# A diffusion layer on one Trainium2 core: sums of squares and weight block sums given to VectorE

## The chip, the cores and the metric

The kernel runs on one core of one Trainium2 chip. The time is the device's microseconds (us) for one execution; lower is better. All engines of the core are used: TensorE (PE, with its weight loads PEld), VectorE (DVE), ScalarE (ACT), GpSimd (POOL), and SyncE (SP), which issues most of the DMA transfers.

## What is computed

One layer of a hybrid diffusion backbone, in float32, for 1024 latent tokens and 256 context tokens of 1024 channels:

```python
def rms_norm(x, g):
    return x * lax.rsqrt(jnp.mean(x * x, axis=-1, keepdims=True) + EPS) * g

def swiglu(h, w_in, w_out):                      # w_in 1024 x 5632, w_out 2816 x 1024
    a, b = jnp.split(h @ w_in, 2, axis=-1)
    return (jax.nn.silu(a) * b) @ w_out

x = x + 0.5 * g1 * swiglu(modulate(rms_norm(x, n1), s1, c1), ffn1_w_in, ffn1_w_out)
h = modulate(rms_norm(x, n2), s2, c2)
...                                              # h @ w_in; short convolution; attention; merge; w_out
x = x + 0.5 * g3 * swiglu(modulate(rms_norm(x, n3), s3, c3), ffn2_w_in, ffn2_w_out)
out = rms_norm(x, final_g)                       # the output: latent tokens only
```

The context tokens pass through the first two parts with the same weights. What matters here are the norms (each needs, per token, the sum of the squares of its 1024 channels) and the two products with `w_out` of the feed-forward parts.

## The kernel before, in words

Activations lie transposed: a tile is 128 channels by 512 tokens, so the 1024 latent tokens are two chunks, C0 and C1, of eight tiles each. All instructions go through wrappers of one line (L90), so a profile's line column always says L90 and groups are told by the names of their tiles. A tile framework schedules the instructions, so that neighbours in the program need not be neighbours on an engine.

**The stages.** FFN1 (input product, SwiGLU; the hidden values `hid` go to DRAM and come back), FFN1's output product, the mixer's input products, attention, the merge, `w_out`, FFN2's input product, FFN2's output product with the final norm, and the output.

**The output products, `row_products`.** The product of `w_out` with the hidden values is taken as seven products over 2x2 blocks (Strassen's scheme), in the order 2, 1, 4, 6, 5, 7, 3. Its `groups` are six steps over the 11 k-tiles of 128 rows: five steps of two k-tiles (tiles of 128x2x512) and a last one of a single k-tile (128x512). `operands` yields both factors of a step, each split into a high part rounded by ScalarE (`wh`/`wl` of the weights and `rh` of the hidden values) and the rest, which VectorE makes by a subtraction; the weights' high and low parts lie in the tiles `wl`/`wh` by turns, and the hidden values' in `rh`/`rl`. Each k-tile then takes 12 matmuls of 128x512: four column blocks by three pairs of parts. Three products use sums of weight blocks as their weights: product 5 `s1[k]` = w12 + w22, product 6 `s2[k]` = w11 − s1, and product 3 the same tile with w21 added. `sums(i, g)` makes them ahead of time. For every group the quarter w12 is loaded by SP into a tile `ws`, and GpSimd issues a DMA that adds w22 to it in SBUF (`plus`, an accumulating DMA). In product 4, ScalarE copies −s1 into another tile `ws`, and GpSimd issues a DMA that adds w11 to that; in product 6 a third adds w21 for product 3. Groups 0 to 2 get their s1 in product 1, and groups 3 to 5 in product 4. So GpSimd has three such DMAs per group, 18 in each of the two `row_products`; it issues them in order, and an accumulating DMA follows the one before it once that has landed. Product 4's own weights are w22, in a tile `raw` (three buffers) loaded by `part_of_w`. `halves=True` (FFN2) takes product 3 in two halves of 256 tokens at the end.

**The norms.** ScalarE squares each of the eight channel tiles of a chunk. `square` adds the squares 0 to 6 into one tile, `sq_acc`, by VectorE, and keeps the eighth, `sq`, apart. `rstd_cols` then multiplies each 128 tokens of each such tile with a column of ones on PE (`pt<-ones,sq`, a product of 128x1 that is summed in PSUM), VectorE makes the reciprocal root of it (`rs_a`, `rs_t`, `rs_y`), and `bcast` spreads it by transposes (`ident,rs_y`). `square` serves the mixer's norm of C0 and of C1, and FFN2's norm of C1.

**The end, `final`.** It is called for three chunks of tokens: 512 (C0), 256, and the last 256 (`early`). Of the eight squares of a chunk, C0 adds them in pairs to four tiles; the two others add the first four in pairs and keep the other four, which makes six. Each of these is multiplied with ones for each 128 tokens: 4x4 + 2x6 + 2x6 = 40 products with ones. The values themselves (`yf`) are transposed by PE, scaled by VectorE or ScalarE into `ot`, and stored. `after3` places these steps between the matmuls of FFN2's product 3.

Of the kernel before, what the change touches and what calls it, by code (L numbers as in the profile page):

```python
# [12 lines left out]
AF = mybir.ActivationFunctionType  # L13
# [5 lines left out]
P = 128  # L19
D = 1024  # L20
KD = D // P
# [30 lines left out]
def tile_dit_layer(  # L52
# [44 lines left out]
    act, dve, pool, pe, sp = (Engine(e) for e in (nc.scalar, nc.vector, nc.gpsimd, nc.tensor, nc.sync))  # L97
# [15 lines left out]
    def atile(name, shape=(P, SLOT), dt=F32):  # L113
        return apool.tile(list(shape), dt, tag="A", name=uniq(name))
# [377 lines left out]
    class Winograd:  # L492
# [53 lines left out]
        def square(self, d, ch=C1):  # L546

            accs, n = self.accs.setdefault(ch, []), self.n_squares.get(ch, 0)
            sq = ttile("sq" if n else "sq_acc")
            act.activation(out=sq, in_=self.xs(d, ch), func=AF.Square)  # L550
            if n in (0, KD - 1):
                accs.append(sq)
            else:
                dve.tensor_add(out=accs[0], in0=accs[0], in1=sq)
            self.n_squares[ch] = n + 1
# [270 lines left out]
    def row_products(w, rows, add, after=lambda i, k: None, halves=False):  # L826
# [9 lines left out]


        R, groups = P * rows.n, rows.groups
        s1, s2 = {}, {}

        def block(k, m, lower, right):
            o = k * P + R * lower
# [2 lines left out]
        def part_of_w(*kmlr):  # L845
            t = wpool.tile([P, 2, 512], F32, tag="raw", name=uniq("raw"), bufs=3)[:, : kmlr[1]]
            load(t, block(*kmlr))
            return t

        def plus(t, *kmlr):  # L850
            pool.dma_start(out=t, in_=block(*kmlr), accum_op=ALU.add)
# [14 lines left out]
        def blocks(k):  # L866
            return (rows.t[k, v, c] for v in range(2) for c in range(2))

        def fetches(i, g):
# [5 lines left out]
            elif i == 1:  # L875
                rows.fetch(0, 0, g + 5)
                rows.fetch(0, 1, g + 2)

        def sums(i, g):

            n = len(groups)
            if i == 2 and g >= 2 or i == 1 and g < 2:
                k, _ = groups[g - 2 if i == 2 else n - 2 + g]
                _, _, b21, b22 = blocks(k)
                dve.tensor_sub(out=b21, in0=b21, in1=b22)
            if i == 1 and g or i == 4 and g == 0:
                k, _ = groups[g - 1 if i == 1 else n - 1]
                b11, b12, b21, _ = blocks(k)
                dve.tensor_sub(out=b11, in0=b12, in1=b11)
                dve.tensor_add(out=b21, in0=b21, in1=b11)  # L890
            if i == 1 and g >= 3 or i == 4 and g < n - 3:
                k, m = groups[g - 3 if i == 1 else n - 3 + g]
                s1[k] = atile("ws", (P, 2, 512))[:, :m]
                load(s1[k], block(k, m, 0, 1))
                plus(s1[k], k, m, 1, 1)
            k, m = groups[g]
            b11, b12, _, b22 = blocks(k)
            if i == 4:
                dve.tensor_sub(out=b11, in0=b11, in1=b22)
                s2[k] = atile("ws", (P, 2, 512))[:, :m]  # L900
                act.activation(out=s2[k], in_=s1[k], func=AF.Copy, scale=-1.0)
                plus(s2[k], k, m, 0, 0)
            elif i == 6:
                dve.tensor_add(out=b11, in0=b11, in1=b22)
                plus(s2[k], k, m, 1, 0)
            elif i == 5:
                dve.tensor_sub(out=b12, in0=b22, in1=b12)

        def operands(i, k, m):

            b11, b12, b21, b22 = blocks(k)
            if i in (1, 2, 4):
                left = part_of_w(k, m, i != 1, i == 4)
            elif i == 7:
                left, a21 = part_of_w(k, m, 0, 0), part_of_w(k, m, 0, 1)
                dve.tensor_sub(out=left, in0=left, in1=a21)
            else:
                left = (s1 if i == 5 else s2)[k]
            right = {1: b11, 2: b21, 4: b21, 5: b11, 6: b11, 7: b12, 3: b22}[i]
            for e in range(m):  # L920
                if i != 3:
                    where = ("wl", "wh")[(k + e) % 2], "t"
                else:
                    where = ("kept", "kept") if halves else ("wl", "wh")
                yield parts(left[:, e], where[0]), parts(right[:, e], where[1])
# [150 lines left out]
    for k in range(4):  # L1076
        if k % 2:
            half1.shifted(h0[k][:, 0], k, xh[k])
        else:
            dve.tensor_scalar(  # L1080
                out=h0[k][:, 0], in0=xh[k], scalar1=gain1["l"][:, k : k + 1], scalar2=modl[:, k : k + 1],
# [158 lines left out]
    for d in range(0, KD, 2):  # L1240
# [8 lines left out]
        for e in range(2):  # L1249
            te = t[:, e * CT : (e + 1) * CT]  # L1250
            dve.scalar_tensor_tensor(
                out=te, in0=pt[:, e * CT : (e + 1) * CT], scalar=gate1["c"][:, d + e : d + e + 1], in1=te, op0=ALU.mult, op1=ALU.add
# [78 lines left out]
    for i in range(KD):  # L1331
# [6 lines left out]
        for ch, bg, gc in mixed():  # L1338
# [4 lines left out]
            for j in (0, 2):  # L1343
# [3 lines left out]
                    out=ya, in0=u[:, a + j - 1 : b + j - 1], scalar=col(f"w{j}", i), in1=ya, op0=ALU.mult, op1=ALU.add  # L1347
# [383 lines left out]
    for ch in (C0, C1):  # L1731
        o = ch[1]
        for d in range(KD):
# [7 lines left out]
                out=xs(d, ch), in0=ps, scalar=modl[:, 40 + d : 41 + d], in1=xs(d, ch), op0=ALU.mult, op1=ALU.add  # L1741
# [12 lines left out]
        out=gf[:], in0=cols[:, voff["gf"] : voff["gf"] + 8], scalar1=math.sqrt(D), scalar2=None, op0=ALU.mult  # L1754
    )
    def final(ch, order, early=False):

        s, o, n = ch
        sqs, yk, turned = [], {}, {}
        for i, k in enumerate(order):  # L1760
            sq = ttile("sq", n)
            act.activation(out=sq, in_=xs(k, ch), func=AF.Square)
            if i % 2 and (i < 4 or n == 512):
                dve.tensor_add(out=sq, in0=sq, in1=sqs.pop())
            sqs.append(sq)
            if i % 2 == 0:
                y2 = atile("yf", (P, 2, 512))
            yk[k] = y2[:, k % 2, :n]
            dve.tensor_scalar(out=yk[k], in0=xs(k, ch), scalar1=gf[:, k : k + 1], scalar2=None, op0=ALU.mult)
            yield  # L1770

        def turn(j, half):
            pt = (ps_o if half and not early else ps_s)()
            for i in range(4):
                transpose(pt[:, i * P : (i + 1) * P], yk[half * 4 + i][:, j * P : (j + 1) * P], pinned=early)
            return pt

        if early:
            turned = {(j, half): turn(j, half) for half in (1, 0) for j in range(n // P)}
        rstd = rstd_cols(sqs, n, D)  # L1780
        yield
        for j in range(n // P):
            ot = atile("ot")
            for half in range(2):
                pt = turned.get((j, half)) or turn(j, half)
                oh = ot[:, half * 512 : (half + 1) * 512]
                if half:
                    act.activation(out=oh, in_=pt, func=AF.Copy, scale=rstd[:, j : j + 1])
                else:
                    dve.tensor_scalar(out=oh, in0=pt, scalar1=rstd[:, j : j + 1], scalar2=None, op0=ALU.mult)  # L1790
            sp.dma_start(out=out[0, o + j * P : o + (j + 1) * P, :], in_=ot[:])
            yield
# [94 lines left out]
```

## Time and profile before

| | |
|---|---|
| time, median of 3 runs | 2662.51 us (2657.9 to 2662.89) |
| the profiled execution's own time | 2661.18 us |
| its span in the profile | 2659.4 us |
| mean granted TensorE clock | 0.995 |
| DRAM read and written | 308.88 MB and 69.76 MB |

Times are us unless marked ns. In a group of instructions, "out<-in" are the program's names of the tiles, then shape and count; behind the bar stand busy time and mean ns of one, and behind the second bar the engine's idle time just ahead of them and what ended it. A timeline row gives start and duration, and in brackets the idle time just ahead and the instruction that ended it. The chain of waits is the work that ended last, followed back from the end; in it "issue" is time in which an engine waited for nothing that the profile shows. A table by windows gives for each stretch the busy time and count of each engine, the granted TensorE clock as a share of full speed, the DMA's share and GB/s. One product with ones stands in the trace as two records.

### The profile page before, as it was taken

How to read it: one execution, taken by the hardware profiler on the slowest of the kernel's cores; microseconds unless marked ns; L12 is line 12 of the kernel's file. 1: busy time of each engine (PE TensorE's matmuls, PEld its weight loads, DVE VectorE, ACT ScalarE, POOL GpSimd, SP SyncE). 2: the span in 40 equal slices, each digit the busy share in tenths (PEclk: the TensorE clock that was granted, in tenths of full speed). 3: DMA queues.
4: the chain of work that ended last, by engine and by line, in shares of the span. 5: the costliest groups of instructions: out<-in, count | busy, mean ns of one | idle time of the engine just before them, and what ended most of it. 6: DMA issues, size and time to landing. Idle time of an engine off the chain costs nothing.

```text
span 2659.4 us, 35547 instructions
## 1 busy us (share of the span) xinstructions
PE 2625.4 (99%) x12749; PEld 2187.9 (82%) x12749; DVE 1996.4 (75%) x3361; ACT 1170.4 (44%) x2321; POOL 556.7 (21%) x431
## 2 busy tenths in 40 slices
PE   8999999999999999999999999999999999999998
PEld 6788899888778878888888888888888888888888
DVE  5778976878887899877788676675458876667895
ACT  6533454433443642333345576574235333334453
POOL 0143201221010044333023112141001533230200
PEclk9999999999999999999999999999999999999999
DMA  8656465345974455332522432113525643227841
GB/s 320 203 180 204 139 222 174 108 127 189 323 181 111 130 178 164 115 123 88 192 78 94 91 89 64 32 48 104 162 81 182 190 147 99 80 91 284 187 91 64
DMA packets 368394, 381.03 MB, mean 143 GB/s; under 512 B 19526, under 2 KB 252120, under 8 KB 368216
## 3 DMA queue, kind: packets, MB, share of 16 engines
q1 hardware_dynamic: 357400, 357.22, 41.4%
q0 software_dynamic: 10816, 21.53, 4.9%
q8 instruction: 100, 1.64, 0.3%
q14 instruction: 78, 0.64, 0.1%
HBM read 308.88 MB, written 69.76 MB: 142 GB/s over the span
## 4 chain that ended last, share of the span: by engine, by line
PE 89%; DVE 5%; issue 2%; DMA 2%; ACT 1%; POOL 0%; SPq 0%; DVEq 0%; ACTq 0%; POOLq 0%
PE ps L90 74%; PE po L90 8%; PE pt L90 7%; DVE wl L90 1%; DMA rawm<-in_w_mod_dram 1%; DVE macc L90 0%; DVE r L90 0%; DVE xb L90 0%; DVE nt L90 0%; DVE u L90 0%; DMA xtok<-in_x_dram 0%; DVE rs_t L90 0%; POOL ws L90 0%; DMA ws<-in_ffn_w_out_dram 0%; DVE y L90 0%
## 5 line engine op out<-in xcount | busy, mean ns | idle before, releaser
L90 PE MATMUL ps<-r,wl 128*128 128x512 f32 x5196 | 1204.2, 391 | 6.2 <-DVE wl L90 3.7
L90 PEld LDWEIGHTS ps<-r,wl 128*128 128x128 f32 x5196 | 974.5, 188 | 211.8 <-DVE wl L90 5.4
L90 ACT CAST wl<-raw 128x512 fp32r<-128x512 f32 x287 | 177.6, 619 | 222.5 <-PE ps L90 177.0
L90 ACT CAST wl<-sum 128x512 fp32r<-128x512 f32 x218 | 133.4, 619 | 300.5 <-PE ps L90 221.9
L90 DVE TENSOR_TENSOR wl<-raw,wl 128x512 fp32r<-128x512 f32 x287 | 202.3, 707 | 60.1 <-ACT wl L90 58.5
L90 DVE TENSOR_TENSOR wl<-sum,wl 128x512 fp32r<-128x512 f32 x218 | 195.8, 899 | 31.4 <-ACT wl L90 30.3
L90 POOL TENSOR_TENSOR sum<-raw 128x512 f32<-128x512 f32 x55 | 77.5, 1409 | 665.8 <-DMA raw<-in_w_in_dram 203.9
L90 DVE SCALAR_TENSOR_TENSOR macc<-rawm,silu_c,macc 128x512 f32<-128x512 f32 x178 | 144.9, 832 | 16.0 <-DMA rawm<-in_w_mod_dram 15.5
L90 DVE TENSOR_TENSOR u<-u,ps 128x512 f32<-128x512 f32 x186 | 126.0, 679 | 38.2 <-PE ps L90 38.2
L90 POOL TENSOR_TENSOR sum<-raw,sum 128x512 f32<-128x512 f32 x55 | 80.5, 1464 | 311.0 <-DVE wl L90 311.0
L90 DVE TENSOR_TENSOR pts<-pt,pts 128x512 fp32r<-128x512 f32 x160 | 108.7, 686 | 44.2 <-ACT pts L90 42.5
L90 ACT CAST pts<-pt 128x512 fp32r<-128x512 f32 x160 | 93.2, 594 | 86.7 <-PE pt L90 81.7
L90 DVE TENSOR_REDUCE m<-ps 128x1 f32<-128x512 f32 (+1 forms) x192 | 110.2, 594 | 22.0 <-PE ps L90 21.0
L90 ACT CAST rh<-hid 128x512 fp32r<-128x512 f32 x132 | 81.3, 619 | 100.3 <-PE ps L90 88.5
L90 PE MATMUL ps<-rh,wl 128*128 128x512 f32 x360 | 122.2, 390 | 2.1 <-ACT rh L90 2.1
L90 PE MATMUL ps<-wh,r 128*128 128x512 f32 x384 | 120.7, 392 | 0.0
L90 ACT CAST wh<-raw 128x512 fp32r<-128x512 f32 (+1 forms) x85 | 67.8, 801 | 104.0 <-PE ps L90 74.2
L90 PE MATMUL po<-pts,vh 128*128 128x512 f32 x256 | 110.0, 435 | 0.2 <-ACT pts L90 0.2
L90 DVE TENSOR_TENSOR rl<-hid,rh 128x512 fp32r<-128x512 f32 x132 | 89.9, 684 | 22.6 <-PE ps L90 11.0
L90 PE MATMUL ps<-kl,qs 128*128 128x512 f32 x384 | 104.2, 395 | 0.0
L90 PE MATMUL ps<-rh,wh 128*128 128x512 f32 x300 | 102.3, 389 | 0.0
L90 POOL DMA_DIRECT2D ws<-in_ffn_w_out_dram x36 | 42.3, 1257 | 275.7 <-PE ps L90 85.9
(317 smaller groups left out, 5147.4 us busy)
## 6 DMA issues: line engine op xcount, KB each, us to landing
raw<-in_ffn_w_in_dram SPq DMA_DIRECT2D x130, 512.0 KB
raw<-in_ffn_w_out_dram SPq DMA_DIRECT2D x72, 512.0 KB
raw<-in_w_in_dram SPq DMA_DIRECT2D x61, 512.0 KB
rawm<-in_w_mod_dram SPq DMA_DIRECT2D x104, 256.0 KB
hid<-hd SPq DMA_DIRECT2D x40, 512.0 KB
rawm<-in_w_mod_dram SPq DMA_DIRECT2D x32, 512.0 KB
ws<-in_ffn_w_out_dram POOLq DMA_DIRECT2D x30, 512.0 KB, 6.5
ucd<-uc SPq DMA_DIRECT2D x29, 512.0 KB
```

The source lines that it names most:

```text
L90: inst = getattr(self.engine, name)(*args, **kw)
```

## The change

Three edits, each to sums.

In `square` the eighth square is also added by VectorE, so that each norm has one accumulator where it had two, and four products with ones where it had eight, at three uses.

In `final` all squares of a chunk are added into one tile; the early chunk keeps the last square apart. The products with ones go from 40 to 10 (4x1 + 2x1 + 2x2), VectorE's additions from 8 to 20: three more of 128x512 and nine more of 128x256.

In `row_products` the sum w12 + w22 of the groups 3 to 5 is made by VectorE from product 4's raw tile, where GpSimd's accumulating DMA made it before; that tile holds w22 (`part_of_w(k, m, 1, 1)` in product 4), though the change names it `w11`. −s1 of these groups, with the DMA behind it, is issued one group later, the last one in product 6. GpSimd has 15 accumulating DMAs per call where it had 18, and VectorE three additions more, two of 128x1024 and one of 128x512.

```diff
@@ square
-            if n in (0, KD - 1):
+            if n == 0:
                 accs.append(sq)
             else:
                 dve.tensor_add(out=accs[0], in0=accs[0], in1=sq)
@@ row_products
+        def second_sum(k, m):
+            s2[k] = atile("ws", (P, 2, 512))[:, :m]
+            act.activation(out=s2[k], in_=s1[k], func=AF.Copy, scale=-1.0)
+            plus(s2[k], k, m, 0, 0)
@@ sums(i, g)
                 load(s1[k], block(k, m, 0, 1))
-                plus(s1[k], k, m, 1, 1)
+                if i == 1:
+                    plus(s1[k], k, m, 1, 1)
             k, m = groups[g]
+            if i == 4 and g >= n - 3:
+                dve.tensor_add(out=s1[k], in0=s1[k], in1=w11.pop(k))
             b11, b12, _, b22 = blocks(k)
             if i == 4:
                 dve.tensor_sub(out=b11, in0=b11, in1=b22)
-                s2[k] = atile("ws", (P, 2, 512))[:, :m]
-                act.activation(out=s2[k], in_=s1[k], func=AF.Copy, scale=-1.0)
-                plus(s2[k], k, m, 0, 0)
+                if g < n - 3:
+                    second_sum(k, m)
+                elif g > n - 3:
+                    second_sum(*groups[g - 1])
             elif i == 6:
+                if g == 0:
+                    second_sum(*groups[n - 1])
                 dve.tensor_add(out=b11, in0=b11, in1=b22)
                 plus(s2[k], k, m, 1, 0)
@@ operands, i in (1, 2, 4)
                 left = part_of_w(k, m, i != 1, i == 4)
+                if i == 4:
+                    w11[k] = left
@@ final
             act.activation(out=sq, in_=xs(k, ch), func=AF.Square)
-            if i % 2 and (i < 4 or n == 512):
-                dve.tensor_add(out=sq, in0=sq, in1=sqs.pop())
-            sqs.append(sq)
+            if i and not (early and i == KD - 1):
+                dve.tensor_add(out=sqs[0], in0=sqs[0], in1=sq)
+            else:
+                sqs.append(sq)
```

**GpSimd, FFN1's output product.** These are its accumulating DMAs from the fourth on, before; ws_7020, ws_7067 and ws_7116 are the sums s1 of groups 3 to 5, and the others −s1 and what is added to it, of groups 0 to 5.

```order
L90 DMA ws_7020<-in_ffn_w_out_dram 128x2x512
L90 DMA ws_7024<-in_ffn_w_out_dram 128x2x512
L90 DMA ws_7067<-in_ffn_w_out_dram 128x2x512
L90 DMA ws_7071<-in_ffn_w_out_dram 128x2x512
L90 DMA ws_7116<-in_ffn_w_out_dram 128x512
L90 DMA ws_7120<-in_ffn_w_out_dram 128x2x512
L90 DMA ws_7167<-in_ffn_w_out_dram 128x2x512
L90 DMA ws_7214<-in_ffn_w_out_dram 128x2x512
L90 DMA ws_7250<-in_ffn_w_out_dram 128x512
```

The same place now: ws_7023 to ws_7292 are −s1 and w11 of groups 0 to 5, and the seventh row is the first that adds w21.

```order
L90 DMA ws_7023<-in_ffn_w_out_dram 128x2x512
L90 DMA ws_7069<-in_ffn_w_out_dram 128x2x512
L90 DMA ws_7117<-in_ffn_w_out_dram 128x2x512
L90 DMA ws_7210<-in_ffn_w_out_dram 128x2x512
L90 DMA ws_7247<-in_ffn_w_out_dram 128x2x512
L90 DMA ws_7292<-in_ffn_w_out_dram 128x512
L90 DMA ws_7023<-in_ffn_w_out_dram 128x2x512
```

The three first sums are gone from the queue, so the second sums of groups 0, 1, 2 and 3 stand one, two, three and three places further ahead in it.

**PE, the mixer's norm of C0, in FFN1's product 3.** `ps<-wh,wl` are matmuls of product 3, `ones` the norm's sums, `ident,rs_y` the transposes that spread it, and `ps<-r` the first product that needs it. Before:

```order
L90 MATMUL ps_8008<-wh_8191,wl_8188 128x512 x3
L90 MATMUL ps_8009<-wh_8191,wl_8188 128x512 x3
L90 MATMUL ps_8010<-wh_8191,wl_8188 128x512 x3
L90 MATMUL pt_8048<-ident,rs_y_7992 128x128 x4
L90 MATMUL ps_8011<-wh_8191,wl_8188 128x512 x3
L90 MATMUL ps_8008<-wh_8212,wl_8209 128x512 x3
```

Now, the corresponding place:

```order
L90 MATMUL pt_7982<-ones,sq_acc_7072 128x1 x4
L90 MATMUL ps_8007<-wh_8129,wl_8126 128x512
...
L90 MATMUL ps_8007<-wh_8209,wl_8206 128x512 x2
L90 MATMUL pt_8045<-ident,rs_y_7989 128x128 x4
L90 MATMUL ps_8007<-wh_8209,wl_8206 128x512
L90 MATMUL ps_8008<-wh_8209,wl_8206 128x512 x3
```

The products with ones and the transposes both stand 11 matmuls later in product 3: 39 of its matmuls followed the transposes before, and 28 follow them now. At the norm of C1 the ones stand four matmuls earlier and the transposes where they were; at FFN2's norm of C1 the ones stand six later and the transposes ten.

**PE, the very end.** Its last rows before are the transposes of the early chunk (`yf`) and that chunk's sums of squares:

```order
L90 MATMUL ps_23962<-ident,yf_23935 128x128 x2
L90 MATMUL ps_23962<-ident,yf_23942 128x128 x2
L90 MATMUL pt_23967<-ones,sq_23828 128x1
L90 MATMUL pt_23967<-ones,sq_23913 128x1
L90 MATMUL pt_23967<-ones,sq_23933 128x1
L90 MATMUL pt_23967<-ones,sq_23937 128x1
L90 MATMUL pt_23967<-ones,sq_23940 128x1
L90 MATMUL pt_23967<-ones,sq_23944 128x1
```

Now:

```order
L90 MATMUL ps_23943<-ident,yf_23914 128x128 x2
L90 MATMUL ps_23943<-ident,yf_23923 128x128 x2
L90 MATMUL pt_23948<-ones,sq_23778 128x1
L90 MATMUL pt_23948<-ones,sq_23925 128x1
L90 MATMUL pt_23948<-ones,sq_23778 128x1
L90 MATMUL pt_23948<-ones,sq_23925 128x1
L90 MATMUL po_23884<-ident,yf_23601 128x128 x2
L90 MATMUL po_23884<-ident,yf_23610 128x128 x2
```

Of twelve products with ones at the end four are left, and four transposes of the middle chunk now come behind them.

2 lines of the change are left out of this document (1 added, 1 removed).

## The prediction, made before the change ran

> **What bounds the kernel now.** The page's busy shares and its chain come first.
>
> ```profile
> PE 2625.4 (99%) x12749; PEld 2187.9 (82%) x12749; DVE 1996.4 (75%) x3361; ACT 1170.4 (44%) x2321; POOL 556.7 (21%) x431
> PE 89%; DVE 5%; issue 2%; DMA 2%; ACT 1%; POOL 0%; SPq 0%; DVEq 0%; ACTq 0%; POOLq 0%
> ```
>
> PE is busy nearly all the time, so an edit is worth what it takes off PE or off the few stretches in which PE waits. The largest wait near an edit lies in FFN1's output product, where the chain (start, duration, what) leaves PE:
>
> ```profile
> 764.17 6.02 issue
> ...
> 770.21 5.62 DMA ws<-in_ffn_w_out_dram
> ...
> 775.91 0.63 ACT wh L90
> 776.56 0.69 DVE wh L90
> ...
> 781.68 2.50 PE pt L90 x5
> 784.18 1.18 PE po L90 x3
> ...
> 801.68 30.60 PE ps L90 x135
> ```
>
> GpSimd's accumulating transfer at 770.21 lands, ScalarE and VectorE split what it made, and PE goes on. In PE's timeline this is one of two waits:
>
> ```profile
> 764.98 0.96 PE L90 MATMUL ps<-rh,wl 128*128 128x512 f32 x3 [2.13 <-ACT rh L90]
> 781.68 0.80 PE L90 MATMUL pt<-rl,wl 128*128 128x512 f32 x1 [2.42 <-DVE rl L90]
> ```
>
> GpSimd's timeline shows why the transfer is late. It issues one transfer after another, each when the one before has landed:
>
> ```profile
> 736.12 1.21 POOL L90 DMA_DIRECT2D ws<-in_ffn_w_out_dram  x1 [7.60 <-issue]
> 744.05 1.22 POOL L90 DMA_DIRECT2D ws<-in_ffn_w_out_dram  x1 [6.72 <-PE ps L90]
> 754.97 2.15 POOL L90 DMA_DIRECT2D ws<-in_ffn_w_out_dram  x2 [9.69 <-issue]
> 764.08 1.22 POOL L90 DMA_DIRECT2D ws<-in_ffn_w_out_dram  x1 [6.97 <-issue]
> ```
>
> By GpSimd's order these are the second sum of group 0, the first sum of group 4, the second sum of group 1 with the first of group 5, and the second sum of group 2; that of group 3 is the one at 770.21. Product 6 consumes them as fast as they land.
>
> **FFN1's output product.** Without the three first sums, the second sum of group 1 goes out in the slot at 736.12 instead of 754.97, that of group 2 at 744.05 instead of 764.08, that of group 3 near 755 instead of 770.21: each 15 us or more ahead, against waits of 2.13 and 2.42. Both should go, also if a group's issue one step later gives back 5.4 (24 matmuls of 0.2267, which is 30.60 / 135). What else goes with them, the windows show (PE's granted clock is the third number from the end):
>
> ```profile
> 764.00:766.00 2.00, 1.02 (x4) 0.70 (x5) 1.56 (x3) 1.91 (x4) 1.22 (x1) 1.00 0.08 9
> 782.00:784.00 2.00, 2.00 (x6) 1.52 (x6) 1.93 (x4) 1.75 (x4) 1.22 (x1) 0.50 0.52 93
> 784.00:786.00 2.00, 2.00 (x8) 1.66 (x7) 2.00 (x4) 2.00 (x5) 0.00 (x0) 0.72 0.66 98
> ```
>
> After the wait of 2.42 the clock is halved: the five and three matmuls took 2.50 + 1.18 for 8 × 0.2267 = 1.81, 1.87 more. After the wait of 2.13 it stayed whole. So the sum is −(2.13 + 2.42 + 1.87) = **−6.4**. The Trainium skill, "TensorE: Matmul & The Clock Gate", Part 1, says that the clock drops after an idle window of about 3.4 us, free-running. By its letter neither wait would reach that, and the 1.87 would be no part of what the change takes away: −4.6 here. The trace disagrees in this place, the clock having halved after 2.42, and I go by the trace.
>
> The price is VectorE's. It takes two additions of 128x1024 and one of 128x512, and its timeline shows room:
>
> ```profile
> L90 DVE TENSOR_TENSOR raw<-raw,raw 128x1024 f32<-128x1024 f32 x2 | 2.4, 1219 | 0.0
> 753.49 1.22 DVE L90 TENSOR_TENSOR hid<-hid,hid 128x1024 f32<-128x1024 f32 x1
> 756.29 0.69 DVE L90 TENSOR_TENSOR sq_acc<-sq_acc,sq 128x512 f32<-128x512 f32 x1 [1.58 <-ACT sq L90]
> 764.44 0.69 DVE L90 TENSOR_TENSOR wh<-ws,wh 128x512 fp32r<-128x512 f32 x1 [7.46 <-ACT wh L90]
> ```
>
> 2 × 1.22 + 0.69 = 3.1 us, and VectorE has 1.58 + 7.46 idle at the end of product 4, where they fall. They cost nothing beside that; uncovered, 3.1. Each addition waits for the load of w12, issued three groups (16 us) ahead, and for the raw tile, which product 4 has read by then. Queued behind it on VectorE are the low parts that PE needs next. On SP, one load for product 7 moves behind eight transfers of `x`; product 7 begins two products (60 us) later, so I count nothing. GpSimd's second sums wait for the additions through ScalarE's copy, one group later, which is in the 5.4 above.
>
> In FFN2's output product the same edit finds no wait to take away, and VectorE's and PE's windows there are these (busy time of PE, PEld, DVE, ACT, POOL):
>
> ```profile
> 2484.00:2514.00 30.00, 30.00 (x134) 24.86 (x133) 22.60 (x34) 15.11 (x25) 6.99 (x6) 1.00 0.75 161
> ```
>
> PE is full, VectorE has 7.4 of 30 free, and 3.1 fits: **0**, up to +3.1.
>
> **The norms of the mixer and of FFN2.** Of each eight products with ones (16 records in the chain) four go. The rows are those of C0 with its transposes, of FFN2's C1, and of the kernel's last sum:
>
> ```profile
> 875.34 1.68 PE pt L90 x16
> ...
> 885.12 0.44 PE pt L90 x4
> ...
> 2009.00 1.68 PE pt L90 x16
> 2649.04 2.59 PE pt L90 x24
> ```
>
> That is 0.84 at each of three places, against one VectorE addition of 0.69 where VectorE isn't waited for. But the ones and the transposes have moved. At C0 39 matmuls of product 3 (8.84 us) covered the way from the transposes to the first product with `r`; now 28 do. VectorE's row for the low part of the fourth tile of `r`, and PE's rows at later waits on such tiles, are
>
> ```profile
> 896.04 0.68 DVE L90 TENSOR_TENSOR r<-x,r 128x512 fp32r<-128x512 f32 x1
> 956.14 1.19 PE L90 MATMUL ps<-r,wl 128*128 128x512 f32 x4 [0.67 <-DVE r L90]
> 959.50 12.85 PE L90 MATMUL ps<-r,wl 128*128 128x512 f32 x49 [2.17 <-DVE wl L90]
> 2063.11 1.21 PE L90 MATMUL ps<-r,wl 128*128 128x512 f32 x4 [0.54 <-DVE r L90]
> ```
>
> The fourth tile was ready at 896.72. PE, with the transposes done at 885.56 and 39 matmuls behind them, began the first tile at 894.40 and, at three matmuls each, the low part of the fourth at 896.67: just in time. With 11 × 0.2267 = 2.5 less cover PE waits 2.5 if there was no slack, and 0 if the scheduler's other moves on VectorE make up for it. I take 2.5, since `r` is made in a dense row of VectorE work. C0 and C1 together: −1.7 + 2.5 = **+0.8** (−1.7 to +0.8; and if the clock halves after it, as after 959.50, where 49 matmuls took 12.85 for 11.11, another 1.7). At C1 the transposes stay where they were. At FFN2's C1 the transposes come 10 matmuls later, 2.3, less 0.84: `r` is 1.4 later, and PE already waits there for `r` at 2063.11. −0.84 + 1.4 = **+0.6** (−0.8 to +0.6).
>
> **The final norm.** 30 of 40 products with ones go, 60 records of 2.59 / 24 = 0.108: **−6.4**. PE is the chain without a gap here up to 2651.6. The group for the old products is
>
> ```profile
> L90 PE MATMUL pt<-ones,sq 128*128 128x1 f32 x80 | 9.3, 243 | 0.0
> L90 DVE TENSOR_TENSOR sq<-sq,sq 128x512 f32<-128x512 f32 x4 | 2.7, 680 | 0.0
> L90 DVE TENSOR_TENSOR sq<-sq,sq 128x256 f32<-128x256 f32 x4 | 1.6, 419 | 0.0
> 2604.00:2618.00 14.00, 14.00 (x118) 13.96 (x118) 14.00 (x27) 9.76 (x21) 0.00 (x0) 1.00 0.01 2
> 2618.00:2632.00 14.00, 14.00 (x122) 14.00 (x121) 8.54 (x29) 3.98 (x10) 0.00 (x0) 1.00 0.03 10
> 2632.00:2647.00 15.00, 15.00 (x132) 15.00 (x132) 8.07 (x26) 3.36 (x6) 0.00 (x0) 1.00 0.32 132
> ```
>
> Busy times of records overlap (9.3 × 60 / 80 = 7.0), so I keep the chain's spacing. VectorE takes three additions of 0.680 and nine of 0.419, 5.8 us. It is full up to 2618 and has 29 − 16.61 = 12.4 free in the two windows after that, of which PE's gain takes 6.4: 12.4 − 6.4 − 5.8 = 0.2 is left over. So it hides, barely, if the additions can spread; those of the first chunk fall partly into the full window and push what follows. The early chunk's last square stays apart, so the end waits for no addition more. Four transposes of the middle chunk now stand last on PE; their way out (ScalarE, a store) is no longer than the one through `rs_a` to `ot`.
>
> **The sum.** −6.4 + 0 + 0.8 + 0.6 − 6.4 = −11.4. Against the profiled execution's own 2661.18 that is 2649.8; that execution is 1.3 under the median of 2662.51, from which it would be 2651.1. I put the forecast between them: **2650.5**. With the bounds of the norms (−4 to +1.7) its own range is 2647 to 2654.
>
> **Rivals.**
>
> A. FFN1's wait changes form. VectorE works in order, and an addition that comes late holds back the low parts; the second sums of groups 3 and 4, now behind additions, could again be late. For it: GpSimd's row still spends 6 to 10 us per transfer, and nine follow each other. Against it: the slots are 15 us ahead. It leaves 1.4 of the 6.4: −6.4 in all, 2655.5. That the transfers hadn't bound PE at all, so that the edit doesn't do what it says, gives the same. Chance 0.14.
>
> B. VectorE paces the last stretch. For it: 0.2 left over, and 14.00 of 14.00 at 2604. Against it: the additions are spread over three stretches. PE waits for 5 of the 6.4: 2655.5. Chance 0.10.
>
> C. No new waits at the norms; VectorE's other work shifts as well and `r` comes in time. For it: the order of VectorE around `r` is scheduled anew; against it: the transposes stand later by count. −6.4 − 1.7 − 0.8 − 6.4 = −15.3: 2646.5. Chance 0.12.
>
> D. The 1.87 at half clock stays or returns at another wait, as after a new 2.5 at C0: −11.4 + 1.8 = −9.6, 2652.3. Chance 0.05. It is what the skill's free-running window would allow, as the place of a wait in it would decide.
>
> E, on the other side: the addition of `s1` waits for its load. The loads go through SP's queue and need a free tile `ws`; if w12 lands after VectorE reaches the addition, VectorE stands still with PE's low parts queued behind it. There are six such additions in the two calls. At the price of the row at 781.68, a wait of 2.42 with 1.87 at half clock is 4.3 each: 25.8, so +14.4, 2676. It decides from the fourth: −11.4 + 4 × 4.3 = +5.8. Against it: the loads go out 16 us ahead, and GpSimd's accumulating transfer took the same quarter until now with the same load in front of it. Chance 0.05.
>
> **How the numbers follow.** The forecast has 0.54. About 0.2% (5.3 us) is what a measurement of this kernel can tell from no change; faster by more than that means under 2657.2. The forecast, C and D lie below it, 0.71. A and B lie near it at 2655.5, and I give half of their 0.24 to either side: faster 0.83, same 0.12, slower 0.05. The range takes in C with its bound and A and B with the width of the bounds: 2644 to 2658, which leaves out E and the outer parts of A and B.
>
> **What would show it.** Right: in the new profile PE has no wait for `rl` or `rh` between products 4 and 6 of FFN1's output product, and the granted clock stays at 1.00 there; GpSimd's first second sum goes out about 9 us earlier; the last sum of squares has 8 records where it had 24; PE waits some 2.5 for `r` after the transposes at C0. Wrong: PE waits for VectorE between 2600 and the end, or VectorE waits for a transfer ahead of an addition of `ws`; a time over 2658 would need one of these, and a time under 2644 a gain in a stretch of which nothing here speaks.

## The result, and the profile after

The changed kernel takes 2655.54 us in the median of 12 runs (2649.9 to 2658.48), beside 2662.72 us for the kernel before (2657.9 to 2664.69, 12 runs). The ratio is 0.9968 with an interval of 0.9959 to 0.9976: 8.5 us less, between 6.4 and 10.9; the two medians are 7.2 apart. The forecast was 2650.5, 11.4 less, in the range of 2644 to 2658. The profiled execution took 2655.43 us, with a span of 2653.7.

First the page of the changed kernel: busy shares and the chain of waits by engine.

```profile
PE 2618.7 (99%) x12665; PEld 2178.3 (82%) x12665; DVE 2012.7 (76%) x3382; ACT 1172.7 (44%) x2321; POOL 552.7 (21%) x425
PE 85%; DVE 8%; DMA 2%; issue 2%; ACT 2%; POOL 0%; SPq 0%; DVEq 0%; ACTq 0%; POOLq 0%
```

PE has 84 records fewer (24 and 60, as counted) and 6.7 us less to do; VectorE has 21 instructions and 16 us more, and takes 8% of the chain where it had 5%.

**FFN1's output product.** GpSimd's timeline (start, duration, what, idle time ahead). The first row is the last of the three sums w12 + w22 that GpSimd still makes, the next four are the second sums of groups 0 to 3.

```profile
725.03 1.21 POOL L90 DMA_DIRECT2D ws<-in_ffn_w_out_dram  x1 [9.32 <-DMA ws<-in_ffn_w_out_dram]
734.51 1.23 POOL L90 DMA_DIRECT2D ws<-in_ffn_w_out_dram  x1 [8.27 <-PE ps L90]
742.36 1.21 POOL L90 DMA_DIRECT2D ws<-in_ffn_w_out_dram  x1 [6.62 <-PE ps L90]
748.73 1.22 POOL L90 DMA_DIRECT2D ws<-in_ffn_w_out_dram  x1 [5.16 <-ACT wl L90]
755.24 1.21 POOL L90 DMA_DIRECT2D ws<-in_ffn_w_out_dram  x1 [5.29 <-ACT ws L90]
```

The second sums of groups 1 and 3 go out at 742.36 and 755.24; before they went out at 754.97 and 770.21, in an execution that had reached this place 3.4 us sooner. So they are 16 and 18 us ahead; the second sum of group 0, at 734.51 for 736.12, is 5 ahead. The windows show PE full and its clock (third from the end) whole, where the two waits were:

```profile
764.00:768.00 4.00, 4.00 (x20) 3.30 (x19) 3.20 (x6) 2.20 (x5) 2.11 (x2) 1.00 1.05 391
776.00:780.00 4.00, 4.00 (x20) 3.30 (x19) 4.00 (x8) 1.44 (x3) 0.00 (x0) 1.00 0.69 124
780.00:784.00 4.00, 4.00 (x19) 3.33 (x18) 4.00 (x6) 1.99 (x4) 1.22 (x1) 1.00 0.39 31
```

**The norms.** PE's timeline has new waits: the first two rows at the mixer's C0, the others at FFN2's norm.

```profile
891.82 0.96 PE L90 MATMUL ps<-r,wl 128*128 128x512 f32 x3 [0.81 <-DVE r L90]
893.93 9.61 PE L90 MATMUL ps<-r,wl 128*128 128x512 f32 x41 [1.15 <-ACT r L90]
2051.38 1.26 PE L90 MATMUL ps<-r,wl 128*128 128x512 f32 x3 [0.68 <-ACT r L90]
2053.60 0.73 PE L90 MATMUL ps<-r,wl 128*128 128x512 f32 x2 [0.96 <-DVE r L90]
2054.83 7.09 PE L90 MATMUL ps<-r,wl 128*128 128x512 f32 x30 [0.50 <-ACT wl L90]
```

What VectorE does meanwhile at C0:

```profile
883.77 4.87 DVE L90 TENSOR_TENSOR x<-x,pt 128x512 f32<-128x512 f32 x8 [0.90 <-PE pt L90]
888.56 0.69 DVE L90 TENSOR_TENSOR wl<-raw,wl 128x512 fp32r<-128x512 f32 x1
889.16 0.69 DVE L90 TENSOR_TENSOR r<-x,r 128x512 fp32r<-128x512 f32 x1
889.76 1.41 DVE L90 SCALAR_TENSOR_TENSOR x<-ps,gate_l,x 128x512 f32<-128x512 f32 x2
891.08 0.68 DVE L90 TENSOR_TENSOR r<-x,r 128x512 fp32r<-128x512 f32 x1
891.68 1.40 DVE L90 SCALAR_TENSOR_TENSOR x<-ps,gate_l,x 128x512 f32<-128x512 f32 x2
```

It waits 0.90 for the transposes (`pt`), multiplies eight tiles with them, and only then makes the parts of `r`, with the sums of product 3's last block between them. With 28 matmuls of cover instead of 39, PE gets there first and finds `r` missing. At FFN2's norm the two waits of before, 0.54 and 0.48, are still there behind the new ones, now 0.62 and 0.65.

**The end.** The groups of the products with ones and of the additions, from 2550 on, then the chain's last piece of PE and VectorE's last row, then two windows:

```profile
L90 PE MATMUL pt<-ones,sq 128*128 128x1 f32 x20 | 2.4, 238 | 0.0
L90 DVE TENSOR_TENSOR sq<-sq,sq 128x256 f32<-128x256 f32 x13 | 5.2, 422 | 0.4 <-ACT sq L90 0.4
L90 DVE TENSOR_TENSOR sq<-sq,sq 128x512 f32<-128x512 f32 x7 | 4.8, 693 | 0.0
```

```profile
2645.07 0.80 PE pt L90 x8
...
2648.05 0.75 DVE ot L90
```

```profile
2618.00:2632.00 14.00, 14.00 (x121) 14.00 (x120) 11.61 (x37) 3.26 (x10) 0.00 (x0) 1.00 0.01 2
2632.00:2642.00 10.00, 10.00 (x89) 10.00 (x87) 9.06 (x31) 2.66 (x5) 0.00 (x0) 1.00 0.27 109
```

The last sum has 8 records for 24, and PE is full to its end. VectorE is busy 20.67 of 24 us and has 3.3 left.

### The profile page after: what moved, and what is told of

It reads as the page before. It is cut to its first block, busy times and chain, and to the rows that moved or that the text cites. A ratio compares the mean times of both kernels' runs of the same rounds, so it can differ in the third digit from the quotient of the medians.

```text
span 2653.7 us, 35378 instructions
## 1 busy us (share of the span) xinstructions
PE 2618.7 (99%) x12665; PEld 2178.3 (82%) x12665; DVE 2012.7 (76%) x3382; ACT 1172.7 (44%) x2321; POOL 552.7 (21%) x425
## 4 chain that ended last, share of the span: by engine, by line
PE 85%; DVE 8%; DMA 2%; issue 2%; ACT 2%; POOL 0%; SPq 0%; DVEq 0%; ACTq 0%; POOLq 0%
PE ps L90 70%; PE po L90 8%; PE pt L90 7%; DVE wl L90 1%; DMA rawm<-in_w_mod_dram 1%; DVE u L90 1%; DVE macc L90 1%; DVE r L90 1%; DMA raw<-in_ffn_w_in_dram 1%; POOL sum L90 0%; DVE nt L90 0%; DVE y L90 0%; DVE xb L90 0%; DVE v L90 0%; DVE rs_t L90 0%
## 5 line engine op out<-in xcount | busy, mean ns | idle before, releaser
L90 PE MATMUL ps<-r,wl 128*128 128x512 f32 x5196 | 1208.7, 392 | 11.4 <-DVE wl L90 3.8
L90 DVE TENSOR_TENSOR rl<-hid,rh 128x512 fp32r<-128x512 f32 x132 | 90.4, 687 | 26.7 <-ACT rh L90 16.0
L90 PE MATMUL ps<-y,wc 128*128 128x512 f32 x384 | 97.1, 392 | 0.2 <-DVE g L90 0.2
```

The costliest lines, as they stand in the source:

```text
L90: inst = getattr(self.engine, name)(*args, **kw)
```

## The experiments

Single profiled executions differ by some microseconds in places that no edit touches: from the 50th to the 2950th matmul, for which PE's instructions are the same in all these kernels, they took between 575.3 and 580.6 us. So edits are also compared by stretches: the time between the starts of the same two matmuls of PE, counted without transposes and products with ones, in each trace; the 24 products with `silu_c`, all ahead of the 50th, are left out of the count too. A matmul at full speed is 0.2267, so the first three stretches can't go under 45.3, 79.3 and 68.0 us (the last column ends with the span). The ratios are of the times, each beside the kernel before on the same chip.

| kernel | FFN1's output product, 3550 to 3750 | mixer's norms, 4050 to 4400 | FFN2's norm, 8650 to 8950 | end, from 11350 | ratio to before, interval |
|---|---|---|---|---|---|
| before | 52.2 | 88.8 | 72.2 | 48.9 | |
| before, once more | 50.6 | 89.0 | 74.1 | 48.9 | |
| the change | 45.3 | 89.6 | 75.5 | 42.0 | 0.9968 (0.9959 to 0.9976) |
| the change, once more | 45.3 | 90.8 | 75.5 | 42.0 | 0.9965 (0.9953 to 0.9978) |
| first edit alone | 51.0 | 90.0 | 75.5 | 50.6 | 1.0012 (1.0002 to 1.0021) |
| final norm alone | 50.4 | 88.1 | 74.8 | 42.0 | 0.9978 (0.9969 to 0.9987) |
| block sums alone | 45.3 | 87.4 | 74.7 | 48.9 | 0.9985 (0.9975 to 0.9994) |
| without the first edit | 45.3 | 88.1 | 74.8 | 42.0 | 0.9966 (0.9955 to 0.9976) |
| the same, once more | 45.3 | 90.4 | 73.3 | 42.0 | 0.9965 (0.9951 to 0.9979) |
| eighth square left out | 48.7 | 87.6 | 72.6 | 50.6 | 0.999 (0.9981 to 0.9998) |
| one block sum, group 3 | 45.3 | 88.1 | 74.9 | 48.9 | 0.9979 (0.997 to 0.9987) |
| one block sum, group 5 | 47.9 | 89.1 | 73.3 | 48.9 | 0.9985 (0.9975 to 0.9995) |
| final additions doubled | 45.3 | 89.3 | 74.7 | 49.3 | 0.9977 (0.9969 to 0.9986) |
| first edit at C1 only | 45.3 | 89.0 | 74.9 | 42.0 | 0.9959 (0.9946 to 0.9973) |

From the 8950th to the 11350th matmul, FFN2's input product and most of its output product, each of these took 538.5 us.

**The clock.** Part of the differences is half clock. In every one of these traces the granted clock changes only at moments that lie a whole number of 3.413 us apart. They cut an execution into equal windows, and where these lie against the program differs from one execution to the next. Here are the windows around the second wait of FFN1's output product, first in the first profile of the kernel before (a wait of 2.42), then in its second (2.29):

```profile
778.28:781.69 3.41, 0.99 (x6) 0.49 (x4) 3.41 (x6) 0.00 (x0) 0.03 (x1) 1.00 1.02 160
781.69:785.10 3.41, 3.41 (x8) 2.74 (x9) 3.34 (x6) 2.85 (x6) 1.22 (x1) 0.50 0.51 85
```

```profile
777.61:781.03 3.42, 2.20 (x10) 1.50 (x8) 3.42 (x6) 0.90 (x2) 1.12 (x2) 1.00 0.98 198
781.03:784.44 3.41, 2.34 (x10) 1.94 (x11) 3.41 (x7) 2.02 (x4) 1.22 (x1) 1.00 0.66 117
```

The first wait lies in one window, in which PE is busy 0.99 of 3.41, and the next window is at half clock. The second is cut in two, 1.22 and 1.07, and the clock stays whole. From 600 to 2600 us of the 14 traces, all 16 windows at full clock in which PE stood idle for 1.79 us or more were followed by half clock; of the 17 with 1.5 to 1.77, four were; of those with less, none. A window at half clock costs up to half its length, 1.7 us.

**The theory, T**: the edits act each in its place and add up; the block sums win by GpSimd's queue, the final norm by PE's records, and the first edit loses because the norm's chain gets longer than what covers it. Its rivals are named with each run.

### The first edit alone

```diff
-            if n in (0, KD - 1):
+            if n == 0:
                 accs.append(sq)
```

> The kernel before with the first edit alone: the eighth square added by VectorE, the rest as before. Theory T (the delayed chain of the norm costs more than the products with ones save): the transposes at the mixer's C0 and at FFN2's C1 come 11 and 10 matmuls later, PE waits there as in the changed kernel (0.81 + 1.15 and about 2.4 us more, with some half clock behind), so slower by 3 to 5 us, about 2667 beside 2662.7. Rival R1 (those waits come from the sums edit, since PE reaches the norm 6 us earlier and VectorE doesn't): no new wait here, faster by 2 to 2.5 us (24 records of 0.107), about 2660.

Measured: 2664.84 us, 1.0012 (1.0002 to 1.0021), so 3.2 us slower (0.5 to 5.6). PE's timeline at C0 has the waits of the changed kernel, though the sums edit is not in it:

```profile
891.67 0.97 PE L90 MATMUL ps<-r,wl 128*128 128x512 f32 x3 [0.80 <-DVE r L90]
893.79 9.60 PE L90 MATMUL ps<-r,wl 128*128 128x512 f32 x41 [1.15 <-ACT r L90]
```

R1 falls. The two norm stretches are longer than in the kernels without this edit by 1.3 and 1.3 (90.0 against a mean of 88.7; 75.5 against 74.2). Another 1.6 lies at the end, where the windows show PE busy throughout at a granted clock of 0.88 from 2640 to 2650; the kernel without the eighth square has the same 50.6. There PE doesn't wait, but its 24 records of products with ones for the middle chunk stand in one row of 2.6 us. In these two executions 19 and 24 of them fall into one window of the clock, and the next is at half clock; in the five others with this ending at most 14 to 19 do, and the clock stays whole (at 19 it is seen both ways). So the 1.6 goes by where the windows lie, as far as seven executions show it, and is not the edit's.

### The final norm alone

```diff
-            if i % 2 and (i < 4 or n == 512):
-                dve.tensor_add(out=sq, in0=sq, in1=sqs.pop())
-            sqs.append(sq)
+            if i and not (early and i == KD - 1):
+                dve.tensor_add(out=sqs[0], in0=sqs[0], in1=sq)
+            else:
+                sqs.append(sq)
```

> The kernel before with the edit of the final norm alone. T: 60 records go and VectorE's twelve additions hide, so -6.4 us, about 2656, with no wait of PE after 2380. Rival R2 (VectorE paces the end): PE waits for a sum or for a low part between 2600 and the end, and 1 to 2 us are gained, about 2661.

Measured: 2656.24 us, 0.9978 (0.9969 to 0.9987), 5.9 us faster; the end takes 42.0 where it took 48.9, with no wait of PE from 2380 to 2645. T holds, R2 falls. FFN1's second wait, untouched here, is in PE's timeline, this time with matmuls at full speed behind it (the windows cut it into 1.27 and 1.17):

```profile
781.25 0.50 PE L90 MATMUL pt<-rl,wl 128*128 128x512 f32 x1 [2.44 <-DVE rl L90]
781.59 0.62 PE L90 MATMUL pt<-rh,wl 128*128 128x512 f32 x2
782.06 0.40 PE L90 MATMUL pt<-rl,wl 128*128 128x512 f32 x1
782.29 0.39 PE L90 MATMUL pt<-rh,wl 128*128 128x512 f32 x1
```

The starts are 0.23 apart; a row's duration overlaps the next.

### The block sums alone

```diff
-                plus(s1[k], k, m, 1, 1)
+                if i == 1:
+                    plus(s1[k], k, m, 1, 1)
...
+            if i == 4 and g >= n - 3:
+                dve.tensor_add(out=s1[k], in0=s1[k], in1=w11.pop(k))
```

The rest of the third edit, the later issue of −s1, is in this run too.

> The kernel before with the block sums of row_products alone. T: both waits of FFN1's output product (2.13 and 2.42) go with the half clock behind the second, -6.4 us, and in FFN2 nothing is won or lost: about 2656. Rival R3 (VectorE's additions cost 3.1 us in FFN2, where VectorE is nearly full): -3.3 us, about 2659, and FFN2's output product is longer from its first matmul to its last.

Measured: 2658.68 us, 0.9985 (0.9975 to 0.9994), 4.0 us faster (1.6 to 6.7). FFN1's stretch is at PE's full speed (45.3). R3's time agrees as well as T's, but its place does not: FFN2's stretch is 538.5 as in every kernel, so VectorE's additions cost nothing there. What was less than T said is FFN1's stretch: without the edit it takes 50.6 on average (five executions, 48.7 to 52.2), so 5.3 was to be had, not 6.4.

### Without the first edit

```diff
-            if n == 0:
+            if n in (0, KD - 1):
                 accs.append(sq)
```

> The changed kernel without its first edit: the eighth square stays apart and has its own products with ones. T: ones and transposes stand where they stood before, PE waits at neither norm, and the two other edits add up: -12.8 us against the kernel before, about 2650, which is 5 us faster than the changed kernel. Rival R1: PE waits for r after the norm of C0 here as well, and the time is 2.5 us over the changed kernel's, about 2658.

Measured: 2653.21 us, 0.9966 (0.9955 to 0.9976), 9.1 us under the kernel before; no wait of PE from 870 to 910, though PE arrives 8 us earlier than in the kernel before. R1 falls here too. The gain of the two edits is 9.1 beside 5.9 + 4.0 = 9.9 from each alone: they add up. T's 12.8 was too much (6.4 to 12.0), and the 5 us under the changed kernel did not show: 9.1 stands beside its 8.5.

### The change, and the change without its first edit, on one chip

> The changed kernel once more, on the same chip as the kernel without its first edit. T by stages: about 2654 (10 us under the kernel before), PE waits at C0 and at FFN2's norm as in its first profile. It is here as the yardstick for the next run.

> The changed kernel without its first edit, on the same chip as the changed kernel. T: 2.4 us under the changed kernel (1.7 from the stretch with the mixer's norms and 0.7 from FFN2's). Rival R5 (the first edit is worth nothing either way, and the difference of the stages is that of single executions): the two agree within 1 us.

Measured: 2654.41 and 2653.54 us, both 0.9965 of the kernel before (0.9953 to 0.9978; 0.9951 to 0.9979). R5 stands by the times: 0.9 us between the medians is no difference that five runs can show, and T's 2.4 is not shown. By the traces the first edit's waits are there, in the same size, in each of its three executions; the gain from leaving it out is 2 to 3 us in the stretches and is not shown in the time.

### The eighth square left out

```diff
-            if n in (0, KD - 1):
+            if n == 0:
                 accs.append(sq)
+            elif n == KD - 1:
+                pass
             else:
                 dve.tensor_add(out=accs[0], in0=accs[0], in1=sq)
```

> The kernel before with the eighth square of the three norms left out altogether (no product with ones, no addition): the norms lack an eighth of their channels. It separates PE's saving from the longer chain. The transposes at C0 stand where they stood before, those at FFN2's C1 six matmuls later. T (the wait comes from the longer chain through VectorE): no wait at C0, the stretch with the mixer's norms 1.7 us shorter than before, FFN2's by 0 to 0.8, about 2660.5. Rival R4 (the wait comes from PE arriving earlier, whatever the chain): PE waits for r at C0 here too, about 1 us, and the time stays at 2662.

Measured: 2660.05 us, 0.999 (0.9981 to 0.9998), 2.7 us faster. PE has no wait at C0, where the stretch took 87.6 and FFN2's 72.6. These are 1.1 and 1.6 under the means without the edit, so PE's saving by itself is worth about what was counted (24 records, 2.6 us); that the time agrees is partly chance, since in its profile the end is 1.6 longer. R4 falls. At C0 it is the longer chain that turns the saving into a loss: the addition, or the transposes that stand 11 matmuls later with it; no run has one without the other. At FFN2's norm the place alone does a part, since PE waits there in this run as well (0.60, 0.65 and 0.48), with the transposes six matmuls later and no addition.

### The kernel before, once more

> The kernel before once more, for a second profile of it. T: the two waits of FFN1's output product are there again (about 2 and 2.4 us), but half clock need not follow: its stretch takes 50 to 52 us. FFN2's first products take 72 us as in the first profile if that is the kernel's own, and 74.8 as in the three runs without the first edit if single executions differ by that much.

The rows of the second wait in this second profile of the kernel before, from PE's timeline and from the windows:

```profile
782.10 0.50 PE L90 MATMUL pt<-rl,wl 128*128 128x512 f32 x1 [2.29 <-DVE rl L90]
```

```profile
782.00:784.00 2.00, 1.90 (x8) 1.58 (x9) 2.00 (x5) 1.58 (x4) 1.22 (x1) 1.00 0.53 94
784.00:786.00 2.00, 2.00 (x10) 1.63 (x10) 2.00 (x3) 2.00 (x5) 0.00 (x0) 1.00 0.76 72
```

The wait is there, the half clock behind it is not, as the clock's windows above have it. And FFN2's norm took 74.1 where the first profile had 72.2: that one was the shortest of all, so that a comparison of the two first profiles alone overstates what the first edit costs there (3.3 instead of 1.3).

### One block sum by VectorE: the first, and the last

The kernel before with one group's sum given to VectorE; first group 3:

```diff
-                plus(s1[k], k, m, 1, 1)
+                if i == 1 or k != groups[n - 3][0]:
+                    plus(s1[k], k, m, 1, 1)
...
+            if i == 4 and g == n - 3:
+                dve.tensor_add(out=s1[k], in0=s1[k], in1=w11.pop(k))
```

> The kernel before, with the block sum of one group alone (the first of the three, group 3) made by VectorE, and its second sum issued in the same group as before. GpSimd's second sum of group 1 then stands one slot further ahead (744 instead of 755), and all behind it. T (GpSimd's one-at-a-time queue is what PE waits for): one slot of 7 to 10 us is more than the waits of 2.1 and 2.4, so both go, FFN1's stretch takes 45 to 46 us where it took 50 to 52, and the time is about 2657. Rival R7 (it takes all three additions, or the second sums' issue a group later): a wait of 1 us or more stays for either group.

and the same with group 5 (`n - 1` for `n - 3`), whose second sum is issued in product 6:

> The kernel before, with the block sum of the last group alone (one k-tile, group 5) made by VectorE. Its place on GpSimd is behind the second sum of group 1. T: the second sum of group 1 goes out where it did, so the first wait (2.1) stays; those of groups 2 and 3 go out one slot earlier, so the second wait (2.4) goes. FFN1's stretch takes 47.5 to 48.5 us, the time is about 2660. Rival R7: both waits stay, 50 to 52 us.

Measured for group 3: 2658.87 us, 0.9979 (0.997 to 0.9987), 5.6 us faster. GpSimd's rows are the last first sum of product 1, the second sum of group 0, the first sum of group 4, and the second sum of group 1 with the first of group 5:

```profile
719.16 1.21 POOL L90 DMA_DIRECT2D ws<-in_ffn_w_out_dram  x1 [9.95 <-DMA ws<-in_ffn_w_out_dram]
726.10 1.23 POOL L90 DMA_DIRECT2D ws<-in_ffn_w_out_dram  x1 [5.73 <-ACT ws L90]
734.87 1.21 POOL L90 DMA_DIRECT2D ws<-in_ffn_w_out_dram  x1 [7.53 <-PE ps L90]
742.02 2.17 POOL L90 DMA_DIRECT2D ws<-in_ffn_w_out_dram  x2 [5.94 <-ACT rh L90]
```

Both waits are gone, and the stretch is at full speed: one large transfer less at the head of the queue does all that three do. T holds and R7 falls.

Measured for group 5: 2661.18 us, 0.9985 (0.9975 to 0.9995), 4.0 us faster by the ratio and 2.8 by the medians. Its rows are the first sum of group 4 and the second sums of groups 1 and 2, then PE's two waits:

```profile
746.73 1.22 POOL L90 DMA_DIRECT2D ws<-in_ffn_w_out_dram  x1 [6.22 <-PE ps L90]
757.31 1.21 POOL L90 DMA_DIRECT2D ws<-in_ffn_w_out_dram  x1 [9.36 <-PE ps L90]
765.39 1.22 POOL L90 DMA_DIRECT2D ws<-in_ffn_w_out_dram  x1 [6.87 <-issue]
```

```profile
766.29 0.96 PE L90 MATMUL ps<-rh,wl 128*128 128x512 f32 x3 [0.60 <-ACT rh L90]
781.76 0.50 PE L90 MATMUL pt<-rl,wl 128*128 128x512 f32 x1 [1.21 <-DVE rl L90]
```

The stretch's 47.9 is what T said, but not as T said it. The second sum of group 2 still goes out 8.1 us after that of group 1 (9.1 between 754.97 and 764.08 before): the small first sum of group 5 had no slot of its own, it went out together with the second sum of group 1 (the row with x2). Without it that sum goes out alone, and both waits shrink, to 0.60 and 1.21, instead of one of them going. Group 5 differs from group 3 in its place and in its size, and the sum of group 4, large and between them, was not moved alone; so place and size are not told apart.

### The final additions doubled

The kernel without the first edit, with an addition behind each of the final norm's, into a tile that nothing reads:

```diff
                 dve.tensor_add(out=sqs[0], in0=sqs[0], in1=sq)
+                dve.tensor_add(out=sq, in0=sqs[0], in1=sq)
```

> The changed kernel without its first edit, with each addition of the final norm followed by one more of the same size, whose result nothing reads: 5.8 us more of VectorE work in the last 60 us. In the changed kernel VectorE is busy 20.67 of the 24 us from 2618 to 2642, so 3.3 are free. T (VectorE's room at the end is used up to within a few us): PE waits for VectorE after 2600 and the end comes 2 to 3 us later, about 2656 against 2653.4. R6 (there is no room left, as the 0.2 in the prediction has it): 5.6 us later, 2659. R8 (the additions find room ahead of 2604, where VectorE stands idle 12 of 14 us): no wait, 2653.4.

Measured: 2657.84 us, 0.9977 (0.9969 to 0.9986), beside 0.9965 and 0.9966 without it: about 3 us of the gain are gone by the ratios, and 2.4 to 3.2 by the medians, each beside the kernel before on its chip. But the run adds more than its expectation says. All 20 additions are doubled, not the 12 that the change brought: 7 of 128x512 and 13 of 128x256, 10.2 us where 5.8 were counted. In the profile PE waits, and what it waits for last hangs on VectorE:

```profile
2635.60 3.13 PE L90 MATMUL ps<-kept,kept 128*128 128x256 f32 x24 [0.78 <-DVE x L90]
2645.23 0.65 PE L90 MATMUL po<-ident,yf 128*128 128x128 f32 x4 [1.41 <-ACT ot L90]
```

With two shorter ones, 0.42 and 0.67, these are 3.3 us of waits where there were none. R8 falls. With 10.2 us, T's rule (what goes beyond the 3.3 free) gives 6.9 and R6's 10.2. R6 falls; T's sign is right by the waits, and its size is not shown: the intervals of the ratios leave anything from nothing to some 7 us. The last stretch grew by 7.3 in the profiled execution, the slowest of the 12, which runs at half clock from 2645.9 on.

### The first edit at C1 only

```diff
-            if n == 0:
+            if n == 0 or (n == KD - 1 and not (self.plain and ch == C1)):
                 accs.append(sq)
```

> The changed kernel with its first edit at the mixer's C1 only; the eighth squares of C0 and of FFN2's C1 stay apart. Ones and transposes of C0 stand where they stood before; at C1 the ones stand 12 and the transposes 18 matmuls later than before. T (what counts is the cover that is left): 0.84 less on PE, and r of C1 comes up to 18 x 0.2267 - 0.84 = 3.2 us later, so the stretch from the transposes of C1 on is 0 to 2.4 us longer than without the edit. R9: no new wait, 0.8 us under the kernel without the edit, 2652.6.

Measured: 2652.27 us (6 runs), 0.9959 (0.9946 to 0.9973). It is the lowest ratio of all, but its interval overlaps that of the change, so it is not shown to be faster. The stretch of the mixer's norms, 89.0, lies among the kernels without the edit (87.4 to 90.4); by the times T and R9 can't be told apart. The trace leans to T: the clock is whole in this stretch, and the three others without the edit at whole clock took 87.4 to 88.1.

## Why the prediction came out as it did

The direction and the mechanisms were right, and the time lies in the range. The gain was 2.9 us smaller than forecast, 8.5 for 11.4, and the forecast lies just outside the interval (6.4 to 10.9). Two of its signs came out smaller: GpSimd's first second sum is 5 us earlier for some 9, and PE's waits at C0 are 1.96 for some 2.5. By steps:

**FFN1's output product, −6.4: measured −5.3.** The queue was the cause, as argued: the group 3 run moves it by one transfer and both waits go. The part that was mis-sized is the half clock, 1.87. The prediction took it as bound to the wait of 2.42 and set the trace against the rule. It is not bound: the same wait of 2.29 in the second profile of the kernel before, and one of 2.44 in the run of the final norm alone, had the clock whole behind them; each was cut in two by the clock's windows, where that of 2.42 lay in one. The Trainium skill, "TensorE: Matmul & The Clock Gate", Part 1, calls the window free-running, and that part of the rule is borne out here: where a wait falls decides. That the idle time must be about 3.4 long is not, since 1.79 to 2.44 in a window of 3.41 was enough in all 16 cases. An average would have been between −4.6 and −6.4. That one accumulating transfer follows another only when it has landed held for the large ones alone, as the group 5 run showed.

**FFN2's additions, 0: measured 0.** The stretch took 538.5 with and without them.

**The norms, +0.8 and +0.6: measured +1.4 and +1.3.** These are means of three executions with the edit beside nine and ten without; at the mixer's norms the two overlap (89.6 to 90.8, and 87.4 to 90.4), at FFN2's they do not (75.5, and 72.2 to 74.9). This is where the sum was furthest off, 1.3 in all. That PE would wait at C0 for want of cover was right, and the waits of 0.81 + 1.15 are near the 2.5. What the term left out is what comes behind a wait: in the change's second profile the 41 matmuls behind the second wait took longer,

```profile
890.80 11.23 PE L90 MATMUL ps<-r,wl 128*128 128x512 f32 x41 [1.15 <-ACT r L90]
```

```profile
892.00:894.00 2.00, 2.00 (x6) 1.62 (x5) 2.00 (x4) 2.00 (x5) 0.00 (x0) 0.50 0.00 1
```

11.23 for 9.61, at half clock, which the bounds had (1.7) and the value had not. Here 0.81 and 1.15 lay in one window of the clock, in the change's first profile they were cut. At FFN2's norm the 1.4 for the delay stood for the one place at 2063.11. PE waits at three more, 0.68 + 0.96 + 0.50, and in all 3.4 us, for 1.0 and 1.5 in the two profiles of the kernel before.

**The final norm, −6.4: measured −6.9.** By records, 0.115 each for the 0.108 counted, and without a new wait. VectorE's room was 3.3 us, where the prediction had 0.2 left over: of the 5.8 us of additions 4.1 came into the windows from 2618 on, and these shrank from 29 to 24 us and not by 6.4. That the room was nearly used up is right: the run with 10.2 us more of additions has 3.3 us of waits.

**The sum** of what the stretches show is −5.3 + 1.4 + 1.3 − 6.9 = −9.5, within the interval of what was timed. **Rivals**: A and B fell by the traces, with no wait left in their places; C fell by the waits at C0; D was right in its mechanism, half clock turning up at another wait, in one of the change's two executions; E fell, since no addition of `ws` waits for a load. In the groups of the changed kernel from 2400 to 2600, as in FFN1, they stand without idle time ahead:

```profile
L90 DVE TENSOR_TENSOR ws<-ws,raw 128x1024 f32<-128x1024 f32 x2 | 2.4, 1218 | 0.0
L90 DVE TENSOR_TENSOR ws<-ws,raw 128x512 f32<-128x512 f32 x1 | 0.7, 685 | 0.0
```

## What to carry to other kernels

A chain that feeds PE has a cover, the matmuls between what starts the chain and what needs its end; before PE's small products are moved to another engine, count that cover, since 0.84 us saved here cost 1.3 where the chain grew by an addition and its place in the order moved. In a queue of transfers that PE waits for, try first to take out a large one at its head: here one of three did what all three did, and the small one at the end about half. And where PE is the bound, wide sums on a neighbour with room are worth 0.1 us per record that they take off it, until that room is used up: at this kernel's end 12 more additions hid, and 20 more on top of them made PE wait 3.3 us.

## What the runs showed of the hardware

- The granted clock is set window by window, 3.413 us each, and it is PE's idle time within a window that matters, not the length of a wait. With 1.79 us or more the next window was at half clock (16 of 16), with 1.5 to 1.77 sometimes (4 of 17), with less never. So 2.42 in one window halved it, and 2.44 and 2.29, cut in two, did not; 0.81 + 1.15 at C0 did so in one of three executions, in which both lay in one window.
- A row of 24 records of products with ones (128x1), 2.6 us without a gap, halved the clock behind it where 19 and 24 of them fell into one window; with 14 to 19 of them in one it did not, in five executions.
- An accumulating transfer of one k-tile (256 KB) goes out beside one of 512 KB without a slot of its own; without it ScalarE could use the transfer of 512 KB 7.8 us after its issue where it was 8.8, and PE waited 0.60 for 2.13.
- Ahead of all edits the same instructions took 575.3 to 580.6 us in single executions, so that a single pair of profiles can't tell changes of a few microseconds unless they are compared by stretches.
